# A two-layer encoder trunk: roots of the last head pair as a power on GpSimd, an early table load and halved gelu, four places in the planned order

## The chip, the cores and the metric

The kernel runs on one core of a Trainium2 chip. The metric is the time of one execution on the device, in microseconds (us). A core has five engines with a queue each, which run side by side and wait for one another through semaphores: TensorE (PE in the profile; its weight loads are shown apart as PEld), VectorE (DVE), ScalarE (ACT), GpSimd (POOL) and SyncE (SP), which here issues nearly all transfers (DMA) between main memory and the core. The instructions of one queue are executed in the order in which they stand there.

## The reference

The input is x, 1024 tokens by 1024 channels in float32. The trunk has two layers, each `x = x + mixer(RMSNorm(x))`, and a final RMSNorm. The first layer's mixer has two branches from one projection; the change lies mostly in them.

```python
def mixer_ab(h, w_in, ..., glu_w, glu_b, w_out):
    proj = h @ w_in
    u_s5, g_s5, q, k, v, g_ret = jnp.split(proj, cuts, axis=-1)
    y_s5 = s5_mixer(u_s5, ..., glu_w, glu_b)
    y_s5 = y_s5 * jax.nn.silu(g_s5)
    ...
    y_ret = retention(q, k, v).astype(h.dtype) * jax.nn.silu(g_ret)
    return jnp.concatenate([y_s5, y_ret], axis=-1) @ w_out
```

At its end, `s5_mixer` (a diagonal state-space recurrence) takes a gelu of its y and then a gated linear unit, the GLU of this text: `y = gelu(y); y = y * sigmoid(y @ glu_w + glu_b)`. `retention` turns q and k by position (rotary: `x1*cos - x2*sin`, `x1*sin + x2*cos`), forms decayed scores inside a chunk and a carried state between chunks for 8 heads, and normalises each head's output over its 128 channels, `(out - mu) * rsqrt(var + EPS)`. The second layer's mixer is a Conformer convolution: `a, b, g = split(h @ w_in)`, `u = a * sigmoid(b)`, a causal convolution of width 31 along the tokens, LayerNorm, `silu`, times `silu(g)`, and `@ w_out` (mm_oc in the kernel).

## The kernel before, in words

Channels lie on the 128 partitions and tokens in the free dimension, in two halves of 512. To keep float32's precision, each operand of a product is split into a high and a low part (names ending in h and l, xh and xl, wh and wl), and TensorE makes three products for one: L231 wh·xh, L232 wh·xl, L233 wl·xh (`mm3`; for v the same three stand at L1192 to L1194 and L1216 to L1218). A weight block of 128 x 1024 takes three steps: SP loads wf (512 KB, L218), ACT casts it to wh (L220), POOL or DVE subtracts to get wl (L221). There are three buffers for each. A block of the last layers is split once and its low part kept in main memory (`lo_woc`); the second half of the tokens then loads wl directly (`low_load`).

In time: the S5 kernel and the gated projections run to about 270 us, then four head **pairs** of retention (to about 560 us), with the S5 branch's gelu and the sums for the GLU woven in; then the GLU (about 530 to 630), the output projection, and the second layer to 1136.

For one pair, `retention` does this. `ret_proj` makes k and q (mm_k, mm_q) and turns them: SP loads a copy with halves swapped (kswp, qswp), POOL multiplies raw and swapped by the tables (L1158, L1160), DVE adds (L1161, krot and qrot). q's table, `ropeq`, has one buffer of 1 MB for all pairs, so the next pair's table (L1135) can be loaded only when the last qswp product has read the old one. `ret_values` (pair 0: `ret_values_wide`, for all heads, eight weight blocks v0_0_0 to v0_1_3) makes v, which ACT evacuates from the banks (L1195, L1220). `y_pass` takes two blocks of the S5 output per pair: SP loads yp (L1034), ACT takes the gelu (L1038), SP stores yn_d; DVE makes differences (L1046 to L1049), casts th (L1053), subtracts (L1054), and SP stores both as t_d (L1055, L1056). `glu_sums` loads blocks of the GLU's weight as gs (L1065), adds and subtracts them on DVE (L1069 to L1072) and stores ws_d (L1075). `ret_heads` makes the scores, the state, the outputs ro, their statistics (st, mv), the reciprocal root rs by `rsqrt` (ACT's Sqrt at L530 and DVE's reciprocal at L531), the normalised `on`, which TensorE transposes (rt, L1329), and the gated result grl, stored as yr_d.

The GLU is built from seven products of blocks over the sums and differences (a Strassen-like scheme), 14 weight blocks glu0 to glu13, whose operands are loaded as y11f, y21f, y22f (split on the core: casts at L1339) and yt1 to yt4 (loaded split, L1381). `gated` multiplies a product by tanh (sg, mm_glus, mm_gluy: L1416 on ACT; the sigmoid is written with it), POOL multiplies gate and y (yg, L1408). ACT has one set of function tables at a time; an ACT_TABLE_LOAD stands in its queue where Sqrt, gelu and tanh follow one another.

The order of each queue is not that of the text: a planner with a model of durations orders the program, and three things bind it. `tc.issue_after(ins)` queues what a block traces **on the engine of `ins`** behind `ins` (order only, no wait; on other engines it has no effect). `self.at(priority)` moves a piece. And the table `ORDER` (L41) lists pairs (engine, early, late): the late instruction, by tile name and number, is to be queued behind the early one, for example qswp_0's first product against a wl_v0 block.

## Time and profile before

| | |
|---|---|
| three runs | 1133.12, 1135.58, 1136.41 us; median 1135.58 |
| the profiled execution | 1138.03 us, of which span 1136.2 |
| TensorE clock granted | 0.999 |
| instructions in the span | 17205 |
| main memory | 182.53 MB read, 74.65 MB written, 226 GB/s over the span |

The span is the time from the first to the last instruction in the trace; 1.8 us of the execution lie around it. Busy times are shares of the span. A row of a timeline has start, length, engine, line, operation, tiles and, in brackets, how long the engine had been idle and what ended it; matmul ends are modelled, so starts are the better measure on TensorE.

### The profile page before, as it was taken

To read this page: it belongs to the slowest core of one execution; us is meant where nothing else is said; L and a number is where in the kernel's file an instruction comes from. 1 tells how busy PE (TensorE), PEld (TensorE's weight loads), DVE (VectorE), ACT (ScalarE), POOL (GpSimd) and SP (SyncE) were. 2 spreads that over 40 slices of the span, in tenths; PEclk is the share of its full clock that TensorE was granted. 3 is DMA by queue.
4 is the path that set the end of the run, shared out by engine and by line. 5 is a ranking of instruction groups with operands and counts; after the bars stand their busy time and mean duration, and the time that the engine had idled before them with its cause. 6 is when DMAs were issued, how large, how long until landed. Compare 5 with 4: busy or idle time off the path is not lost.

```text
span 1136.2 us, 17205 instructions
## 1 busy us (share of the span) xinstructions
PE 1117.1 (98%) x6278; PEld 978.9 (86%) x6278; DVE 828.1 (73%) x1470; ACT 498.0 (44%) x731; POOL 647.3 (57%) x456
## 2 busy tenths in 40 slices
PE   9999999999999999999999999999999999999997
PEld 7888888888888889898888888888888888888886
DVE  6973966777417469587569632599999899999734
ACT  6412433333223221323436523555535677446773
POOL 2059999888127344232475011589544568779863
PEclk9999999999999999999999999999999999999999
DMA  9345555553477866959998998565778755357965
GB/s 354 114 124 167 188 185 176 177 172 138 151 245 251 303 212 181 337 168 325 382 372 277 328 330 285 192 237 198 242 252 281 249 195 179 119 179 246 317 229 187
DMA packets 118181, 262.51 MB, mean 231 GB/s; under 512 B 10704, under 2 KB 42320, under 8 KB 117456
## 3 DMA queue, kind: packets, MB, share of 16 engines
q1 hardware_dynamic: 114640, 248.82, 64.9%
q10 hardware_dynamic: 3456, 12.58, 2.8%
q8 instruction: 49, 0.80, 0.3%
q14 instruction: 36, 0.29, 0.1%
HBM read 182.53 MB, written 74.65 MB: 226 GB/s over the span
## 4 chain that ended last, share of the span: by engine, by line
PE 73%; DMA 13%; DVE 7%; ACT 3%; issue 2%; POOL 1%; SPq 1%; POOLq 0%; DVEq 0%; ACTq 0%
PE mm_g L231 7%; PE mm_g L232 7%; PE mm_g L233 7%; PE mm_wo L231 5%; PE mm_wo L233 5%; PE mm_wo L232 5%; PE mm_a L233 2%; DMA yp<-y_d 2%; PE mm_b L232 2%; PE mm_a L231 2%; PE mm_b L233 2%; PE mm_a L232 2%; PE mm_b L231 2%; PE mm_oc L233 2%; PE mm_oc L231 2%; PE mm_oc L232 2%
## 5 line engine op out<-in xcount | busy, mean ns | idle before, releaser
L1626 DVE SCALAR_TENSOR_TENSOR cv<-u,convw,cv 128x512 f32<-128x512 f32 x390 | 267.7, 749 | 5.4 <-ACT cv L1593 3.4
L1587 POOL TENSOR_TENSOR tp<-tp,tp 128x512 f32<-128x512 f32 x64 | 82.4, 1288 | 33.8 <-ACT tp L1586 32.9
L231 PE MATMUL mm_g<-xh,wh_g 128*128 128x512 f32 x256 | 97.9, 382 | 0.0
L232 PE MATMUL mm_g<-xl,wh_g 128*128 128x512 f32 x256 | 97.0, 379 | 0.0
L233 PE MATMUL mm_g<-xh,wl_g 128*128 128x512 f32 x256 | 95.7, 379 | 0.0
L492 POOL TENSOR_TENSOR s1q<-s1q,s1q 128x512 f32<-128x512 f32 x12 | 17.1, 1424 | 79.1 <-ACT s1q L487 79.1
L1586 ACT ACTIVATE tp<-u,convw 128x512 f32<-128x512 f32 x64 | 45.3, 718 | 34.4 <-POOL tp L1587 33.6
L231 PEld LDWEIGHTS mm_g<-xh,wh_g 128*128 128x128 f32 x256 | 48.8, 191 | 6.8 <-issue 0.2
L442 DVE TENSOR_TENSOR gt<-mm_g,R 128x512 f32<-128x512 f32 x32 | 21.9, 686 | 44.7 <-PE mm_g L233 44.6
L233 PEld LDWEIGHTS mm_g<-xh,wl_g 128*128 128x128 f32 x256 | 48.4, 189 | 6.9
L232 PEld LDWEIGHTS mm_g<-xl,wh_g 128*128 128x128 f32 x256 | 48.4, 189 | 6.6
L221 POOL TENSOR_TENSOR wl_glu<-wf_glu,wh_glu 128x1024 fp32r<-128x1024 f32 x14 | 34.0, 2432 | 33.1 <-ACT wh_glu L220 33.1
L233 PE MATMUL mm_oc<-zh,wl_woc 128*128 128x512 f32 (+1 forms) x144 | 51.0, 357 | 1.2 <-DMA wl_woc<-lo_woc 1.2
L232 PE MATMUL mm_oc<-zl,wh_woc 128*128 128x512 f32 (+1 forms) x144 | 51.2, 356 | 0.0
L231 PE MATMUL mm_oc<-zh,wh_woc 128*128 128x512 f32 (+1 forms) x144 | 50.7, 363 | 0.0
L232 PE MATMUL mm_u<-xl,wh_u 128*128 128x512 f32 x128 | 48.3, 381 | 0.7 <-DVE xl L365 0.7
L233 PE MATMUL mm_a<-h1h,wl_ca 128*128 128x512 f32 x128 | 48.6, 380 | 0.3 <-DMA wl_ca<-lo_ca 0.3
L231 PE MATMUL mm_wo<-ysh,wh_wos 128*128 128x512 f32 x128 | 48.9, 382 | 0.0
L231 PE MATMUL mm_g<-h1h,wh_cg 128*128 128x512 f32 x128 | 48.9, 382 | 0.0
L232 PE MATMUL mm_wo<-ysl,wh_wos 128*128 128x512 f32 x128 | 48.5, 379 | 0.0
L233 PE MATMUL mm_wo<-ysh,wl_wos 128*128 128x512 f32 x128 | 48.5, 379 | 0.0
L233 PE MATMUL mm_b<-h1h,wl_cb 128*128 128x512 f32 x128 | 48.5, 379 | 0.0
(533 smaller groups left out, 3601.9 us busy)
## 6 DMA issues: line engine op xcount, KB each, us to landing
wf_g<-w_ab SPq DMA_DIRECT2D x16, 512.0 KB, 5.0
wf_wos<-w_out SPq DMA_DIRECT2D x16, 512.0 KB, 4.5
wf_wor<-w_out SPq DMA_DIRECT2D x16, 512.0 KB, 5.6
wf_cb<-w_c SPq DMA_DIRECT2D x16, 512.0 KB, 4.8
wf_ca<-w_c SPq DMA_DIRECT2D x16, 512.0 KB, 5.6
wf_woc<-w_out_c SPq DMA_DIRECT2D x16, 512.0 KB
wf_v<-w_v SPq DMA_DIRECT2D x12, 512.0 KB
wf_cg<-w_c SPq DMA_DIRECT2D x11, 512.0 KB, 4.5
```

Source lines behind the costliest of these rows:

```text
L221: self.low_made = lo[i].tensor_tensor(wl[:].rearrange(fl)[:, c], wf[:, c], h.bitcast(F32), op=ALU.subtract)
L231: nc.tensor.matmul(ps, wh[:, kb, :], xh, start=start, stop=False, **more)
L232: nc.tensor.matmul(ps, wh[:, kb, :], xl, start=False, stop=False, **more)
L233: self.last_mm = nc.tensor.matmul(ps, wl[:, kb, :], xh, start=False, stop=stop, **more)
L442: nc.vector.tensor_tensor(nat(gt[:, c]), un(ps[:]), nat(self.R[:, c]), op=ALU.mult)
L492: nc.gpsimd.tensor_tensor(a, a, sq[:], op=ALU.add)
L1586: nc.scalar.mul(sk[:], u[:, k:k + HALF], cw[:, nb, k:k + 1])
L1587: gp.tensor_tensor(s0[:], s0[:], sk[:], op=ALU.add)
L1626: v.scalar_tensor_tensor(dst[:], *tap, accs_[i][:], op0=ALU.mult, op1=ALU.add)
```

## The change

Five things are written:

- `rsqrt` for pair 3 (`pool=pair == 3`): the four rs of the last pair (heads 6 and 7, two halves) are made by a multiply-add on DVE and a power of −0.5 on POOL, 128x4 each, instead of Sqrt on ACT and reciprocal on DVE. `rsqrt` now returns the POOL instruction there, so `last_rs` of pair 3 is one of POOL's, and the two `issue_after(self.last_rs.ins)` in the GLU (the first weights, the first tanh) no longer tie anything on ACT.
- For pairs 1 to 3 gelu's table is loaded right behind the last root of the pair before (`preload_act_table_set` in `issue_after`).
- For pairs 1 to 3 the gelu of 128x1024 is two of 128x512.
- `ORDER`: the first qswp product of pair 0 is tied behind the split of block v0_1_0 in place of v0_0_1; the split ysl2_0 on DVE behind the sum gu2_2; the third matmul of mm_oc2 (second half of tokens), the first that reads its wl, behind the ninth of mm_oc0.

```diff
     ('DVE', ('cv6_0', 23), ('h1l0_1', 0)),
-    ('Pool', ('qswp_0', 0), ('wl_v0_0_1', 0)),
+    ('Pool', ('qswp_0', 0), ('wl_v0_1_0', 0)),
+    ('DVE', ('ysl2_0', 0), ('gu2_2', 0)),
+    ('PE', ('mm_oc2_1_0', 2), ('mm_oc0_1_0', 8)),
 )
...
             nc.vector.tensor_scalar(dst, src, scale, EPS, op0=ALU.mult, op1=ALU.add)
-            nc.gpsimd.tensor_tensor(dst, dst, self.mhalf[:, :dst.shape[1]], op=ALU.pow)
+            return nc.gpsimd.tensor_tensor(dst, dst, self.mhalf[:, :dst.shape[1]], op=ALU.pow)
...
-                nc.scalar.activation(yn[:], yt[:].rearrange("p i m -> p m i"), AF.Gelu_apprx_tanh)
+                for m in ((slice(0, 64), slice(64, P)) if k in (1, 2, 3) else (slice(0, P),)):
+                    nc.scalar.activation(yn[:, m], yt[:, :, m].rearrange("p i m -> p m i"), AF.Gelu_apprx_tanh)
...
                     held.enter_context(self.tc.issue_after(self.last_rs.ins))
+                    nc.scalar.preload_act_table_set("gelu_apprx_tanh_and_others")
...
-                self.last_rs = self.rsqrt(rs[:], mv[:, :, 1])
+                self.last_rs = self.rsqrt(rs[:], mv[:, :, 1], pool=pair == 3)
```

What the planner makes of it is more than the diff says. Lines are two to four higher in the changed kernel (L218 is L220, L1160 is L1164, and so on).

**POOL, the values of pair 0.** Splits wl_v of the eight weight blocks and the rotary products qswp. Before:

```order
L221 TENSOR_TENSOR wl_v_0_2_3409<-wf_v_0_2_3407,wh_v_0_2_3408 128x1024
L1160 TENSOR_TENSOR qswp_3370<-qswp_3370,ropeq_3238 128x512 x2
L221 TENSOR_TENSOR wl_v_0_3_3439<-wf_v_0_3_3437,wh_v_0_3_3438 128x1024
L221 TENSOR_TENSOR wl_v_1_0_3469<-wf_v_1_0_3467,wh_v_1_0_3468 128x1024
L221 TENSOR_TENSOR wl_v_1_1_3499<-wf_v_1_1_3497,wh_v_1_1_3498 128x1024
```

Now:

```order
L223 TENSOR_TENSOR wl_v_0_2_3409<-wf_v_0_2_3407,wh_v_0_2_3408 128x1024
L1164 TENSOR_TENSOR qswp_3370<-qswp_3370,ropeq_3238 128x512
L223 TENSOR_TENSOR wl_v_0_3_3439<-wf_v_0_3_3437,wh_v_0_3_3438 128x1024
L223 TENSOR_TENSOR wl_v_1_0_3469<-wf_v_1_0_3467,wh_v_1_0_3468 128x1024
L1164 TENSOR_TENSOR qswp_3370<-qswp_3370,ropeq_3238 128x512
L223 TENSOR_TENSOR wl_v_1_1_3499<-wf_v_1_1_3497,wh_v_1_1_3498 128x1024
```

One of the two products has moved behind two splits. On DVE, one of the two qrot sums moved with it, behind the second th cast.

**SP, the same stretch.** wf_v_1_1 to wf_v_1_3 are the last v weights, ropeq the next pair's table, wf_k the next pair's k weight. Before:

```order
L218 DMA wf_v_1_1_3497<-w_v 128x1024
L1135 DMA ropeq_3897<-rope_q 128x2048
L1065 DMA gs_0_3383<-w_glu 128x2x512
L218 DMA wf_v_1_2_3536<-w_v 128x1024
L1075 DMA ws_d<-gs_1_3393 256x1x512
L1055 DMA t_d<-th_0_3674 128x1024
L218 DMA wf_v_1_3_3566<-w_v 128x1024
L1056 DMA t_d<-yn_3662 128x1024
L1075 DMA ws_d<-gs_1_3392 256x1x512
L1075 DMA ws_d<-gs_0_3383 256x1x512
L1075 DMA ws_d<-gs_0_3382 256x1x512
L218 DMA wf_k_3596<-w_ab 128x1024
```

Now:

```order
L220 DMA wf_v_1_1_3497<-w_v 128x1024
L220 DMA wf_v_1_2_3536<-w_v 128x1024
L1078 DMA ws_d<-gs_1_3393 256x1x512
L1058 DMA t_d<-th_0_3674 128x1024
L220 DMA wf_v_1_3_3566<-w_v 128x1024
L1059 DMA t_d<-yn_3662 128x1024
L1078 DMA ws_d<-gs_1_3392 256x1x512
L1139 DMA ropeq_3897<-rope_q 128x2048
L1058 DMA t_d<-th_0_3679 128x1024
L1068 DMA gs_0_3383<-w_glu 128x2x512
L1059 DMA t_d<-yn_3667 128x1024
L220 DMA wf_k_3596<-w_ab 128x1024
```

The table and gs_0 went from ahead of wf_v_1_2 to behind wf_v_1_3, ahead of wf_k; two ws_d went behind wf_k, two t_d ahead of it.

**ACT, pair 3's roots and the first tanh.** gu are copies of the GLU's first products, wh_glu casts of its weights, sg the first tanh. Before:

```order
L1443 COPY gu_1_5521<-mm_glu_5529 128x512
L530 ACT_TABLE_LOAD
L530 ACTIVATE rs_0_5356<-mv_0_5347,epst 128x4
L530 ACTIVATE rs_0_5374<-mv_0_5365,epst 128x4
L530 ACTIVATE rs_1_5410<-mv_1_5401,epst 128x4
L530 ACTIVATE rs_1_5428<-mv_1_5419,epst 128x4
L220 CAST wh_glu_5579<-wf_glu_5578 128x1024
L1416 ACT_TABLE_LOAD
L1416 ACTIVATE sg_0_5600<-mm_glu_5528,hgb 128x512
```

Now:

```order
L1447 COPY gu_1_5530<-mm_glu_5538 128x512
L222 CAST wh_glu_5588<-wf_glu_5587 128x1024
L1420 ACTIVATE sg_0_5609<-mm_glu_5537,hgb 128x512
L222 CAST wh_glu_5638<-wf_glu_5637 128x1024
L1420 ACTIVATE sg_0_5633<-mm_glu_5538,hgb 128x512
```

Both table loads and the four roots have left ACT. Their successors, four TENSOR_TENSOR of 128x4 at L530, stand on POOL behind the first yg product and ahead of the split of this same wh_glu.

In pairs 1, 2 and 3 the load of gelu's table stands right behind the last root on ACT (pair 1: the same place as before; pair 2: four v evacuations earlier; pair 3: the same place, but without the wait for yp). In the GLU, SP's load of glu6 went from ahead of the eight yt4 loads to behind them, that of glu8 from ahead of one yg and the eight yt1 loads to behind them, and the last y22f and the first yr0f came ahead of the load of glu11. On TensorE, the first transposes rt of pair 3 stand four matmuls later; in mm_oc, six matmuls of the next block of zh and zl stand ahead of mm_oc2's first with wl.

## The prediction

> **What bounds the kernel now.** I read the page's table of engines first, then the waits of TensorE, longest first (engine, line and tile that waited, what it waited for, us in total, times, longest).

> ```profile
> PE 1117.1 (98%) x6278; PEld 978.9 (86%) x6278; DVE 828.1 (73%) x1470; ACT 498.0 (44%) x731; POOL 647.3 (57%) x456
> ...
> PE mm_glu L231 <- ACT sg L1416: 1.6, 1, 1.6
> PE mm_v L1217 <- POOL wl_v L221: 1.5, 2, 1.2
> PE mm_oc L233 <- DMA wl_woc<-lo_woc: 1.2, 1, 1.2
> PE mm_v L1192 <- ACT v L1195: 1.1, 1, 1.1
> ...
> PE mm_glu L231 <- ACT v L1195: 0.9, 1, 0.9
> PE mm_wo L231 <- ACT yr0h L1339: 0.9, 1, 0.9
> PE mm_glu L231 <- DVE mm_gluz L1477: 0.7, 1, 0.7
> ...
> PE mm_k L233 <- POOL wl_k L221: 0.6, 1, 0.6
> ```

> TensorE works 1117.1 of 1136.2 us and the diff leaves its 6278 matmuls as they are, so the change can only win these short waits or put new ones in their place. The eight rows shown sum to 8.5 us, and the edits aim at all of them but yr0h and, by their own words, wl_k. A 512-column matmul follows its predecessor every 0.2157 us though its row shows 0.38, so a wait of the list costs 0.15 to 0.25 us more than it says; below I use the distance between two starts, less 0.2157 (0.11 for 256 columns).

> **1. The rotary product of pair 0 (350 to 384 us).** Rows: start, length, engine, line, tile.

> ```profile
> 350.46 2.51 POOL L1160 TENSOR_TENSOR qswp<-qswp,ropeq 128x512 f32<-128x512 f32 x2 [1.40 <-DMA gs<-w_glu]
> 352.93 8.36 POOL L221 TENSOR_TENSOR wl_v<-wf_v,wh_v 128x1024 fp32r<-128x1024 f32 x3
> ...
> 354.19 0.38 PE L1216 MATMUL mm_v<-wh_v,xh 128*128 128x512 f32 x1
> 355.78 0.48 PE L1217 MATMUL mm_v<-wl_v,xh 128*128 128x512 f32 x1 [1.22 <-POOL wl_v L221]
> ...
> 372.26 1.05 ACT L220 CAST wh_v<-wf_v 128x1024 fp32r<-128x1024 f32 x1 [8.45 <-DMA wf_v<-w_v]
> 380.10 1.05 ACT L220 CAST wh_k<-wf_k 128x1024 fp32r<-128x1024 f32 x1 [6.79 <-DMA wf_k<-w_ab]
> ...
> 381.22 2.37 POOL L221 TENSOR_TENSOR wl_k<-wf_k,wh_k 128x1024 fp32r<-128x1024 f32 x1 [5.00 <-ACT wh_k L220]
> ...
> 383.64 0.48 PE L233 MATMUL mm_k<-xh,wl_k 128*128 128x512 f32 x1 [0.60 <-POOL wl_k L221]
> ...
> 372.78 7.22 DMA wf_k<-w_ab
> ...
> 374.00:384.00 10.00, 9.40 (x48) 8.01 (x47) 1.35 (x3) 3.52 (x6) 4.59 (x2) 1.00 1.03 383
> ```

> One of two qswp products (2.51 / 2 = 1.26 us) leaves the place ahead of wl_v_0_3 and goes behind wl_v_1_0. wl_v_0_3 then starts 1.26 us earlier, at 351.7, and is ready near 354.4 instead of 355.7: the wait of 355.78 − 354.19 − 0.22 = 1.38 us goes. The qswp is itself needed late, so its own delay is free.

> But TensorE's next lock in this stage is wl_k, and that one is set by SP's queue. Its chain has no slack: wf_k is issued at 372.78 and lands 7.22 us later (the chain of waits), ACT casts it at 380.10, POOL splits it from 381.22 to 383.59, TensorE goes on at 383.64. The rope table's load (ropeq, 1 MB) can't be issued before the second qswp has read the old table, so it moves from the head of this queue to behind the fourth weight of v, and with it gs_0. Between that weight and wf_k there stood t_d and three ws_d, all of 512 KB; now t_d, ws_d, the table (two such pieces), t_d, gs_0, t_d. With wf_k itself it is 5 pieces before and 8 now. In 374 to 384 the queue is full (share 1.03, 383 GB/s), which is 0.524 MB / 383 GB/s = 1.37 us a piece. Before, the five took from the cast of the fourth weight, 372.26, to that of wf_k, 380.10: 7.84 us. Now eight take 8 × 1.37 = 10.96, from a start that I let come 0.5 us earlier because wf_v_1_2 no longer queues behind the table: 371.7 + 11.0 = 382.7, against 380.0. With the same cast and split behind it TensorE resumes **2.7 us later** than before; the 1.38 us won is lost inside that. Bounds: wf_k's issue moves up by about 0.9 us (two ws_d fewer ahead of it); if the queue had room for all that is new, −0.9. A piece more: +4.1.

> **2. Pair 2's gelu (465 to 470 us) and 3. pair 3's (500 to 530 us).**

> ```profile
> 465.84 1.28 ACT L1038 ACT_TABLE_LOAD   x1 [4.97 <-DMA yp<-y_d]
> 467.14 1.98 ACT L1038 ACTIVATE yn<-yp 128x1024 f32<-128x1024 f32 x1
> 469.02 1.19 ACT L1195 ACTIVATE v<-mm_v,Rtok 128x256 f32<-128x256 f32 x3
> ...
> 500.15 1.28 ACT L1038 ACT_TABLE_LOAD   x1 [0.91 <-DMA yp<-y_d]
> 501.44 2.05 ACT L1038 ACTIVATE yn<-yp 128x1024 f32<-128x1024 f32 x1
> ...
> 528.39 0.62 ACT L1339 CAST y21h<-y21f 128x512 fp32r<-128x512 f32 x1 [6.08 <-DMA y21f<-yn_d]
> 528.92 0.83 ACT L1195 ACTIVATE v<-mm_v,Rtok 128x256 f32<-128x256 f32 x2
> ```

> In pair 2 ACT idles 4.97 us for yp, then loads the table, and the v evacuation that TensorE's bank waits for stands behind load and gelu. The load now fits into that idle time: 1.28 us off a wait of 1.13 in the list (1.30 by starts). Two halves instead of one whole add some 0.1 us (an estimate: the 1.98 of one whole is my only row). I take **−1.15**, bounds −1.3 and −0.8.

> In pair 3 the last root ends 0.91 us ahead of the load, so the gelu moves up by 0.9 us plus at most the rest of 1.28. What waits on it is long: yn_d, the t_d and y21f loads, then the cast y21h at 528.39, which holds v at 528.92 and so TensorE (0.94 in the list, 1.10 by starts). Queue and chain move together: **−0.9**, bounds −0.3 (if the full queue from 512 us on keeps its own pace) and −1.1.

> [...]

> **4. Pair 3's roots (545 to 556 us).**

> ```profile
> 546.41 0.30 ACT L530 ACTIVATE rs<-mv,epst 128x4 f32<-128x4 f32 x1
> ...
> 553.08 1.28 ACT L1416 ACT_TABLE_LOAD   x1
> 554.37 0.69 ACT L1416 ACTIVATE sg<-mm_glu,hgb 128x512 f32<-128x512 f32 x1
> ...
> 547.07 1.28 POOL L1408 TENSOR_TENSOR yg<-yg,yn 128x512 f32<-128x512 f32 x1
> ...
> 551.84 1.04 PE L1329 MATMUL rt<-ident,on 128*128 128x128 f32 x8
> ...
> L1829 POOL TENSOR_TENSOR fo<-x,RF 128x256 f32<-128x256 f32 x4 | 2.8, 726 | 4.9 <-ACT RF L1819 4.9
> ```

> With no Sqrt left, the Sqrt table's load, four roots and the tanh table's load leave ACT; sg can start when its product is there, instead of 554.37. TensorE's longest wait (1.6 in the list, 1.75 by starts) goes: **−1.75**. The price moves to POOL: four powers of 128x4 behind yg, which ends at 548.35, and ahead of the next wl_glu. The trace has no power. From 128x256 at 0.73 and 128x512 at 1.28 the line through no columns stands at 0.18 us, which is the lower bound; 1.28 us, seven times that and the length of a whole 128x512 product, is my upper one. At 1.28 the first two powers end at 550.9, the `on` products of DVE about 1.5 us later, and the first transposes, which ran from 551.84 and stand four matmuls (0.86) later now, begin at 552.7: no wait. I take 0.3 us, near the rows' small end, and nothing for it.

> **5. The GLU's weights and 6. its tail (557 to 601 us).**

> ```profile
> 557.00:592.00 35.00, 35.00 (x168) 30.71 (x167) 20.04 (x25) 12.82 (x19) 25.44 (x15) 1.00 1.03 383
> ...
> 568.21 7.94 DMA yt1h<-t_d
> 576.21 5.32 DMA yg<-gs_d
> ...
> 576.11 1.04 ACT L220 CAST wh_glu<-wf_glu 128x1024 fp32r<-128x1024 f32 x1
> ...
> 577.23 2.45 POOL L221 TENSOR_TENSOR wl_glu<-wf_glu,wh_glu 128x1024 fp32r<-128x1024 f32 x1 [0.33 <-ACT wh_glu L220]
> ...
> 585.01 0.38 PE L233 MATMUL mm_glu<-yt4h,wl_glu 128*128 128x512 f32 x1
> ...
> 590.19 0.62 ACT L1339 CAST y22h<-y22f 128x512 fp32r<-128x512 f32 x1 [2.99 <-DMA y22f<-yn_d]
> ```

> TensorE never waits from 557 to 592, but the DMA queue is full there. The planner now puts the ninth weight, glu8, behind one yg and the eight yt1 loads. The first of these lands at 568.21 + 7.94 = 576.15, the load behind the last at 576.21 + 5.32 = 581.53: 5.38 us for eight, 0.67 each, so glu8 lands some 6 us later, near 580.9 (0 to 0.9 earlier with step 3). Cast 1.04 and split 2.45 give 583.5 to 584.4. Before, TensorE wanted this split at 585.01 and it was ready at 579.68; having won 0.9 + 1.75 in steps 3 and 4, which the full queue doesn't follow, it wants it at 582.4. So of that gain **+1.4** comes back (bounds 0 and +2.5). In return the last y22f goes out about 3 us earlier; its cast at 590.19 holds DVE's chain up to mm_gluz, TensorE's 0.7 (0.88 by starts): **−0.9** (0 to −1.0).

> **7. mm_oc (1084 us).**

> ```profile
> 1081.08 4.19 DMA wl_woc<-lo_woc
> ```

> The third matmul on this weight waits for 1085.27. Six others now stand ahead of it, 6 × 0.2157 = 1.29 us, whose operands another chunk has ready by then: **−1.3** (−0.8 to −1.4).

> Sum: +2.7 − 1.15 − 0.9 − 1.75 + 1.4 − 0.9 − 1.3 = **−1.9 us**. The profiled execution took 1138.03, 2.45 us above the median of the runs, 1135.58; so a profile of the changed kernel near 1136.1, and a median of 1135.58 − 1.9 = **1133.7 us**.

> **The rivals.** A, the give-backs don't come: the rope table finds room, since the queue was only part busy before 374, and glu8 is in time. Then terms 1 and 5 are −0.9 and 0, and the sum is −6.9: 1128.7 us. For it speaks that only two waits, each inside one queue, stand against it; against it the share of 1.03. B, the power is dear on POOL. At 3 us each the first two end at 548.35 + 6 = 554.35, the first transposes wait about 3 us (555.8 for 552.7); powers three and four end at 560.35, and `on` and the second transposes lose 2.2 us more: +5.3, in sum +3.4, or 1139.0 us. From there on it is slower. Nothing but the rows' linear shape speaks against it, since no row has this operation. C, the queues swallow the rest: the table costs +4.1, glu8 +2.5 and pair 3 wins 0.3 only; +1.2 in sum, 1136.8 us. D, the planner's move does less than it says, as in pair 2 if yp should land later: within 1 us of the forecast, so it is counted with it.

> **Numbers.** Differences under 0.3% (3.4 us) are what the three runs, 1133.12 to 1136.41, can't tell from no change. Forecast with D 0.48, A 0.26, C 0.14, B 0.12. The forecast's own range is −5 to +1 us; I put 0.14 of its 0.48 past −3.4. Faster 0.26 + 0.14 = 0.40, same 0.34 + 0.12 (C without its worst) = 0.46, slower 0.12 + 0.02 = 0.14. The range goes from A's 1128.7, a little below, to C with half of B: 1128.3 to 1138.0 us.

> **What would show it.** Right: no wait of mm_v on wl_v at 355; wf_k landing near 382.7 and mm_k waiting about 4 us for wl_k; no table load between 545 and 557 and sg at once behind its product; a new wait of mm_glu on wl_glu (or wh_glu) near 582; none of mm_oc on lo_woc. Wrong: mm_k waiting less than 1 us (rival A), a power's row over 1.3 us with rt waiting (B), waits of mm_glu over 3 us in all (C). A wait at a place that none of these edits touches would make the sum itself wrong.

## The result and the profile after

| | before | changed |
|---|---|---|
| runs | 22, 1131.82 to 1138.12 us | 22, 1133.20 to 1143.46 us |
| median | 1134.56 us | 1138.45 us |
| ratio, 95% interval | 1 | 1.0034 (1.0024 to 1.0044) |
| mean granted clock over the runs | 0.9987 (the 30 runs beside e1 to e4) | 0.9968 |
| the profiled execution, its span | 1138.03, 1136.2 | 1140.53, 1138.8 |

The change makes the kernel slower by 0.34%, where 1133.7 us were forecast. The waits of TensorE in the changed kernel (what it waited for, us in total, times, longest):

```profile
PE mm_k L233 <- ACT wh_k L222: 3.2, 1, 3.2
PE rt L1333 <- DVE on L1325: 1.5, 1, 1.5
...
PE mm_k L235 <- POOL wl_k L223: 1.0, 1, 1.0
PE mm_glu L233 <- ACT v L1199: 0.7, 1, 0.7
...
PE mm_oc L235 <- DMA wl_woc<-lo_woc: 0.6, 1, 0.6
...
PE mm_glu L235 <- POOL wl_glu L223: 0.2, 1, 0.2
...
PE mm_v L1196 <- ACT v L1199: 0.2, 1, 0.2
```

Gone are the waits on wl_v, sg, mm_gluz and yr0h; new are one of 3.2 us on wh_k and one of 1.5 us of the transposes. That is less waiting in sum than before, and yet the span is 2.6 us longer, so part of the loss is not in this list. The chain of waits, then the timeline of TensorE behind the late weight:

```profile
373.99 8.68 DMA wf_k<-w_ab
...
383.86 0.48 PE L233 MATMUL mm_k<-xh,wh_k 128*128 128x512 f32 x1 [3.18 <-ACT wh_k L222]
...
386.30 0.79 PE L235 MATMUL mm_k<-xh,wl_k 128*128 128x512 f32 x1 [0.97 <-POOL wl_k L223]
386.88 0.63 PE L233 MATMUL mm_k<-xh,wh_k 128*128 128x512 f32 x1
387.31 0.63 PE L234 MATMUL mm_k<-xl,wh_k 128*128 128x512 f32 x1
387.74 0.63 PE L235 MATMUL mm_k<-xh,wl_k 128*128 128x512 f32 x1
...
393.53 0.66 PE L1259 MATMUL kv<-v,kt 128*64 128x128 f32 x8
```

wf_k lands at 373.99 + 8.68 = 382.67, as predicted. But behind the wait the matmuls follow each other every 0.43 us instead of 0.2157. Windows of 4 us show it too (the column before the last two is the granted clock):

```profile
380.00:384.00 4.00, 0.82 (x7) 0.51 (x5) 3.37 (x5) 1.23 (x2) 0.11 (x1) 1.00 1.09 369
384.00:388.00 4.00, 2.92 (x10) 2.06 (x11) 0.69 (x1) 3.07 (x5) 3.10 (x2) 0.68 1.03 393
388.00:392.00 4.00, 4.00 (x10) 3.10 (x10) 0.00 (x0) 1.99 (x2) 2.39 (x2) 0.50 0.75 230
392.00:396.00 4.00, 4.00 (x49) 3.38 (x49) 1.22 (x4) 0.33 (x1) 1.47 (x1) 0.96 0.92 320
```

TensorE ran at half clock until about 392 us. The clock missing in the three windows from 384, weighed by their lengths (0.32 x 4 + 0.50 x 4 + 0.04 x 4), is 3.4 us of work, so the clock stood at half for 6.8 us, a part of it idle. The same products, from this third one of mm_k (386.30) to the first kv (393.53), take 7.23 us; in the kernel before they take 4.30 (383.64 to 387.94). Where the difference of the two profiles arises is read from the start of the matmul with the same number, counted from the program's beginning, in both:

| place | before | changed | difference |
|---|---|---|---|
| values of pair 0, behind wl_v_0_3 | 357.40 | 355.52 | −1.9 |
| behind mm_k's first bank, pair 1 | 388.11 | 393.70 | +5.6 |
| behind pair 2's gelu | 470.53 | 474.72 | +4.2 |
| behind the first sg | 556.08 | 558.26 | +2.2 |
| at the second transposes of pair 3 | 558.46 | 562.48 | +4.0 |
| GLU, behind mm_gluz | 602.84 | 605.73 | +2.9 |
| the last matmul | 1129.96 | 1132.45 | +2.5 |

The gelu's table and the powers, first on ScalarE's timeline, then on GpSimd's and TensorE's:

```profile
503.28 1.28 ACT L1105 ACT_TABLE_LOAD   x1
504.71 2.13 ACT L1041 ACTIVATE yn<-yp 128x512 f32<-128x512 f32 x2
...
552.11 2.01 POOL L530 TENSOR_TENSOR rs<-rs,mhalf 128x4 f32<-128x4 f32 x2
558.75 1.98 POOL L530 TENSOR_TENSOR rs<-rs,mhalf 128x4 f32<-128x4 f32 x2 [4.63 <-DVE rs L529]
...
562.48 0.77 PE L1333 MATMUL rt<-ident,on 128*128 128x128 f32 x5 [1.47 <-DVE on L1325]
```

DVE's `on` products wait for the first powers:

```profile
553.17 1.37 DVE L1325 TENSOR_SCALAR on<-ro,mv,rs 128x128 f32<-128x128 f32 x4 [2.22 <-POOL rs L530]
```

A power of 128x4 takes 1.0 us. Pair 3's halves take 2.13 together where the whole took 2.05.

### The profile page after: what moved, and what is told of

Its sections match the earlier page's. It is cut to its first block, busy times and chain, and to the rows that moved or that the text cites. A ratio compares the mean times of both kernels' runs of the same rounds, so it can differ in the third digit from the quotient of the medians.

```text
span 1138.8 us, 17216 instructions
## 1 busy us (share of the span) xinstructions
PE 1121.3 (98%) x6278; PEld 981.2 (86%) x6278; DVE 828.2 (73%) x1470; ACT 494.8 (43%) x731; POOL 652.0 (57%) x460
## 4 chain that ended last, share of the span: by engine, by line
PE 74%; DMA 12%; DVE 6%; issue 2%; ACT 2%; POOL 1%; SPq 1%; POOLq 0%; DVEq 0%; ACTq 0%
PE mm_g L233 7%; PE mm_g L234 7%; PE mm_g L235 7%; PE mm_wo L235 5%; PE mm_wo L234 5%; PE mm_wo L233 5%; DMA yp<-y_d 3%; PE mm_b L234 2%; PE mm_b L233 2%; PE mm_a L233 2%; PE mm_a L235 2%; PE mm_b L235 2%; PE mm_a L234 2%; PE mm_oc L235 2%; PE mm_oc L234 2%
## 5 line engine op out<-in xcount | busy, mean ns | idle before, releaser
L233 PE MATMUL mm_g<-xh,wh_g 128*128 128x512 f32 x256 | 97.9, 382 | 0.0
L233 PEld LDWEIGHTS mm_g<-xh,wh_g 128*128 128x128 f32 x256 | 48.8, 191 | 6.8 <-issue 0.2
L233 PE MATMUL mm_oc<-zh,wh_woc 128*128 128x512 f32 (+1 forms) x144 | 50.8, 363 | 0.0
L233 PE MATMUL mm_wo<-ysh,wh_wos 128*128 128x512 f32 x128 | 49.0, 383 | 0.0
L233 PE MATMUL mm_g<-h1h,wh_cg 128*128 128x512 f32 x128 | 48.9, 382 | 0.0
L233 PE MATMUL mm_a<-h1h,wh_ca 128*128 128x512 f32 x128 | 48.5, 379 | 0.0
```

What stands on the lines that cost most here:

```text
L233: nc.tensor.matmul(ps, wh[:, kb, :], xh, start=start, stop=False, **more)
```

## The experiments

Three theories run through them. **C**: the late weight makes TensorE wait, and the wait lowers its clock. **W**: only the waiting counts. **R**: the roots and the reordered GLU are the cause.

**e1, the qswp entry alone, and e2, all the rest.** e1 is the kernel before with

```diff
-    ('Pool', ('qswp_0', 0), ('wl_v0_0_1', 0)),
+    ('Pool', ('qswp_0', 0), ('wl_v0_1_0', 0)),
```

and e2 the changed kernel with the same line turned back.

> The kernel before with the one entry for qswp moved and nothing else. Theory C (the late weight wf_k of pair 1 makes TensorE wait over 3 us, and that wait lets its clock fall to half for some 6 us): the wait of mm_k on wh_k comes as in the changed kernel, 3 us, behind it 512-column matmuls 0.43 us apart up to about 392 us, and the whole is 4 to 6 us slower than before (ratio 1.0035 to 1.005). Rival R (the powers on GpSimd and the GLU's reordered loads cost the time, and the clock is the same with or without them): within 1.5 us of before.

> The changed kernel with only the qswp entry put back. Theory C: no wait of mm_k over 1 us, clock 0.998 or more, 2 to 3.5 us faster than before (ratio 0.997 to 0.998), since what is left of the change won 3.1 us by the end of its profile behind 394 us. Rival R: still slower than before, 1 to 4 us.

e1: median 1139.24 against 1134.86, ratio 1.0049 (1.0029 to 1.0069), mean clock 0.9967. e2: 1133.13, 0.9990 (0.9978 to 1.0002), mean clock 0.9989. Theory R falls: the qswp entry alone costs as much as the whole change loses. e1's profile differed from the expectation in one point: mm_k waited 0.47 and 0.98 us there, not 3, at full clock (1.00 from 376 to 400 us), and the half clock (0.50 from 524 to 526) stood behind a 2.2 us wait of mm_v at 523 us. What e2 wins is half of what was expected, and its interval holds 1.

**e3 and e8, the weight ahead of the table.** The changed kernel with one entry more, in e8 with both of these:

```diff
     ('Pool', ('qswp_0', 0), ('wl_v0_1_0', 0)),
+    ('SP', ('ropeq_1', 0), ('wf_k1', 0)),
+    ('SP', ('gs1_0', 0), ('wf_k1', 0)),
```

> The changed kernel with one more entry: the rope table's load (1 MB) behind wf_k on SP, so two pieces of 1.37 us less ahead of wf_k. Theory C: wf_k lands near 380.0 instead of 382.7, mm_k waits under 2 us in all, the clock stays at 1.00 from 384 to 394 us, and the whole is 2 to 4 us faster than before. A theory W (only the waiting counts, the clock doesn't hang on it): 2.7 us less than the changed kernel, so about 1 us slower than before, with the half clock still there.

> e3 with the load of gs_0 (512 KB, one piece) behind wf_k as well. If every piece ahead of wf_k costs 1.37 us: wf_k lands 1.4 us earlier than in e3 (378.1), the wait of mm_k on wl_k (1.2 us by starts in e3) is gone, and the time is 0.5 to 1.2 us under e3's, ratio to before 0.998 to 0.999. If the time hangs on later stages alone: as e3, 0.9993.

e3: 1133.35 against 1134.86, 0.9993 (0.9980 to 1.0006); in its trace wf_k's cast starts at 378.19 and mm_k waited 1.2 us at full clock (1.00 from 376 to 400 us). e8: 1133.39 against 1135.14, 0.9980 (0.9963 to 0.9996); the cast starts at 377.51 and mm_k did not wait. So the loss passes through SP's queue: qswp may stay where the change put it if the table isn't ahead of the weight. The gain of e3 is smaller than expected, as that of e2.

**e9 and e10, only the weight later.** The kernel before with one entry that changes two rows of SP and no other engine; in e10 the number is 2 in place of 3, one row:

```diff
     ('Pool', ('qswp_0', 0), ('wl_v0_0_1', 0)),
+    ('SP', ('wf_k1', 0), ('t_d', 3)),
```

> The kernel before with nothing changed but two rows of SP's queue: wf_k behind the two t_d stores of 512 KB that stood behind it (qswp stays where it was). It lengthens the wait for pair 1's k weight by two pieces, 2.7 us, and touches nothing else. Theory C (a wait of some 3 us halves TensorE's clock for several us): mm_k waits 2.5 to 4 us, half-clock matmuls behind it, mean clock 0.997 or less, and 4 to 6 us slower than before (1.0035 to 1.005). Theory W (only the waiting counts): 2 to 2.7 us slower (1.002) at an unchanged clock.

> The same with one t_d store ahead of wf_k in place of two: 1.37 us more wait. Theory C: the wait stays under 2.3 us, the clock seldom falls, and it is 0.7 to 1.5 us slower than before (1.0005 to 1.0015). Theory W: half of e9, 1 to 1.4 us slower.

e9: 1137.45 against 1134.06, 1.0029 (1.0012 to 1.0046), mean clock 0.9983. e10: 1134.47, 1.0011 (0.9993 to 1.0028), clock 0.9984. Two pieces of 512 KB ahead of one weight cost about 3 us in the runs, with nothing else moved. Here theory W does better: the kernel before stood at 0.9986 beside it, so hardly any of this went through the clock. But both theories expected mm_k to wait, and e9's profile (1135.58, in the faster half of its runs) does not show that: wf_k's cast starts at 377.37 there, earlier than in the first profile of before (380.10), and mm_k waits 0.2 us; its longest waits are two of 1.7 us of mm_v, at 467 and 521 us. Where the slower runs of e9 lose their time was not seen.

**e5, the kernel before a second time.**

> The kernel before once more, for a second profile. Its first profiled execution, 1138.03 us, lies at the top of its 30 runs (1130.6 to 1138.2, median 1134.9). If its waits there (1.75 on sg, 1.40 on lo_woc, 1.38 on wl_v, 1.30 and 1.10 on v, 1.04 on yr0h, by starts) are fixed by the program, they come again within 0.2 us each; if they are an accident of that execution's transfers, some shrink to under half, and the terms of the prediction that rested on them were too large.

1135.57 us. Its waits, and the place of qswp on GpSimd's timeline:

```profile
PE mm_glu L231 <- ACT sg L1416: 1.7, 1, 1.7
PE mm_oc L233 <- DMA wl_woc<-lo_woc: 1.4, 1, 1.4
PE mm_glu L231 <- ACT v L1195: 1.2, 1, 1.2
...
PE mm_v L1192 <- ACT v L1195: 0.7, 1, 0.7
...
346.18 2.51 POOL L1160 TENSOR_TENSOR qswp<-qswp,ropeq 128x512 f32<-128x512 f32 x2 [0.39 <-DMA qswp<-qraw]
```

The waits on wl_v (1.38) and wl_k (0.85) are not in it at all: qswp ran 4.3 us earlier and was through long before the split was wanted, and wf_k's cast started at 374.85, not 380.10. The waits on sg, lo_woc and v are there again. The very wait that the moved qswp was to remove comes in some executions only.

**e11, e12, e15, the changed kernel three times more**, as it stands.

> The changed kernel once more, for a second profile, since its 22 runs reach from 1133 to 1143. If the late weight is fixed by the program: wf_k lands at 382 to 383 again, mm_k waits over 3 us, and the half clock follows. If DVE and GpSimd fall out of step differently from execution to execution (in the trace of e1 the first t_d goes out at 360.5, in that of the changed kernel at 365.7): wf_k lands near 379 in some executions, the wait is about 1.5 us, and the execution takes 1134 to 1136.

> The changed kernel a third time, for a third profile; as the second. The time of each profiled execution should go with the length of the wait of mm_k in it: 1134 to 1136 where the wait is under 2 us in all, 1138 or more where it is over 3.

> The changed kernel a fourth time. So far: wait of mm_k 3.34 + 1.22 us with half clock for 6 us (1140.5), 1.24 + 1.22 with 3.4 us of half clock (1136.7), 1.05 + 1.22 with none (1134.1). Theory C: the three go together here too, and an execution over 1138 us shows half clock at some wait of 2 us or more. Theory W: an execution over 1138 us without half clock.

The waits of mm_k and the window from 384 to 388 us, in the order e15, e11, e12:

```profile
PE mm_k L233 <- ACT wh_k L222: 2.0, 1, 2.0
...
384.00:388.00 4.00, 3.36 (x8) 2.74 (x9) 0.18 (x1) 1.41 (x2) 2.94 (x2) 0.57 0.82 296
```

```profile
PE mm_k L233 <- ACT wh_k L222: 1.1, 1, 1.1
...
PE mm_k L235 <- POOL wl_k L223: 1.0, 1, 1.0
...
384.00:388.00 4.00, 4.00 (x12) 3.20 (x12) 0.00 (x0) 1.19 (x2) 2.35 (x1) 0.61 0.78 243
```

```profile
PE mm_k L235 <- POOL wl_k L223: 1.0, 1, 1.0
PE mm_k L233 <- ACT wh_k L222: 0.9, 1, 0.9
...
384.00:388.00 4.00, 4.00 (x24) 3.27 (x24) 0.00 (x0) 1.11 (x2) 2.37 (x1) 1.00 0.67 224
```

Four profiles of one program, wf_k landing at 382.67, 381.01, 379.80 and 379.72; waits of mm_k on wh_k of 3.2, 2.0, 1.1 and 0.9 us; half clock for 6.8, 3.4, 3.4 and 0 us; and 1140.53, 1136.19, 1136.65 and 1134.06 us. The three go together, but for the order of the middle two. The price of the half clock can be read alone: from mm_k's third product to the first kv, the same products take 7.23, 5.87, 5.99 and 4.30 us, so 2.9, 1.6, 1.7 and 0 us more than the 4.30 of before.

None of the three new profiles came over 1138 us, but the recorded runs bear on theory W. Of the changed kernel's 22, the two slowest, 1142.47 and 1143.46 us, have a mean clock of 0.997 and 0.998, while one of 1136.70 has 0.995. A clock of 0.998 leaves room for one period of 3.4 us at most (e13, with one, shows 0.998, and so does e12, with none: half clock behind the last matmul, 1.7 us of it inside the span in before and 2.4 in the changed kernel, lowers the mean too). A straight line through the 22 gives 0.9 us of time for each us of missing clock, and leaves about three quarters of the spread to something else. So the clock costs about what it is short of, and it is not all that makes these runs slow.

**e4, e6, e13, e14, the wait filled with work.** The changed kernel with products of ones into mm_k's bank, which its first product overwrites:

```diff
                 ps = self.bank(f"mm_{nm}{pair}_{h}", aux=False)
+                for _ in range(12 if (nm, pair, h) == ("k", 1, 0) else 0):
+                    nc.tensor.matmul(ps[:, :P], self.ones[:], self.ones[:], start=True, stop=True)
```

In e4 the planner put the state's products kv ahead of mm_k. From e6 on an entry `('PE', ('kv0_0', 0), ('mm_k1_0', 35))` holds them behind mm_k's first bank.

> The changed kernel with twelve extra products of ones into mm_k's own bank, ahead of its first product (which overwrites them): about 2.6 us of work for TensorE inside the wait for wh_k; transfers and waits are otherwise as they were. Theory C: mm_k's first real product starts as late as in the changed kernel (about 383.9 us), but the products behind it are 0.216 us apart, not 0.43, and the whole is about 3 us faster than the changed kernel (ratio to before 0.999 to 1.002). Theory W: as slow as the changed kernel, 1.0025 to 1.0045.

> As e4 (twelve products of ones, about 2.6 us, ahead of mm_k's first product in the changed kernel), with the state's products kv tied behind mm_k's first bank, as they stand in the changed kernel, since in e4 they had moved ahead of it. Theory C (the wait lowers the clock): mm_k's real products start as late as in the changed kernel, the idle time of TensorE there is under 1.5 us in one piece, mean clock over the runs 0.998 or more against the changed kernel's 0.9968, and the time 1.5 to 3 us under the changed kernel's: ratio to before 1.0005 to 1.002. Theory W (only the waiting counts): 1.003 to 1.004 with the same mean clock as the changed kernel.

> The kernel of e6 (filled wait, order kept) for another profile. Its 12 runs fell into two groups: 4 of 1134.1 to 1136.6 us at a clock of 0.998 to 1.0, and 8 of 1140.9 to 1144.8 at 0.996 to 0.997; its profile was of the first group. In an execution of the second group, theory C1: the half clock stands at mm_k again (384 to 392 us), because the weight came so late that 2.6 us of filling didn't cover it; theory C2: mm_k runs at full clock and a later wait of 2 us or more, made by the transfers that the table's load pushed back (sp on qrot near 435, as in e4's profile, or mm_v near 468 or 522), has the half clock behind it.

> The same kernel a third time, in case e13 falls into the first group; the theories as in e13.

Both expectations of a gain failed. e4: 1144.53, 1.0078 (1.0052 to 1.0104), clock 0.9963. e6: 1141.81, 1.0045 (1.0025 to 1.0066), clock 0.9972, in two groups: 4 runs from 1134.1 to 1136.6 at 0.998 to 1.0, and 8 from 1140.9 to 1144.8 at 0.996 to 0.997. In all three profiles of this kernel (e6 1134.70, e13 1136.63, e14 1135.37) mm_k ran at full clock (products 0.2157 us apart in e6, a clock of 1.00 from 380 to 392 us in e13 and e14); the unfilled kernel did so in one of four. But in e13 the clock fell later, behind mm_v (waits, then windows):

```profile
PE mm_v L1199 <- ACT v L1202: 2.8, 2, 2.2
...
522.00:526.00 4.00, 1.79 (x14) 1.60 (x14) 3.10 (x3) 1.97 (x4) 1.95 (x2) 0.94 0.82 293
526.00:530.00 4.00, 4.00 (x25) 4.00 (x25) 2.43 (x3) 0.00 (x0) 0.00 (x0) 0.64 1.03 410
```

So work in the wait kept the clock at that place in all three, and in one of them it fell at a later long wait. No profile fell in the group over 1140 us; where its clock falls, and whether that is what makes it slow, stays open.

**e7, e16 and e17, the powers.** e7 is e2, and e16 is e8, each with `pool=pair == 3` taken out again; e17 is the kernel before with that argument (and the `return`) alone.

> e2 (the changed kernel with the qswp entry put back) with pair 3's roots on ScalarE again, so only the early gelu table, the halves and the two entries on ysl2 and mm_oc2 remain. If the powers are worth the wait on sg (1.75 us) less the new wait on the first transposes (1.6 us in the changed kernel's profile): within 0.5 us of e2. If they win the whole 1.75: 1.5 to 2 us slower than e2, so ratio to before about 1.000.

> e8 (rope table and gs_0 behind wf_k) with pair 3's roots on ScalarE again: the candidate for the best version. If the powers are worth nothing, as e7 against e2 says: equal to e8, ratio to before 0.9975 to 0.9985, so 2 us faster than before. If the powers win their 1.75 us in this kernel: 0.9995.

> The kernel before with pair 3's roots as powers on GpSimd and nothing else, as the direct measure of that part. Theory D (the wait on sg, 1.75 us, is replaced by a wait of the transposes on the normalised outputs, 0.7 to 1.6 us, and by wl_glu later): 0 to 1 us faster than before, ratio 0.999 to 1.000. As predicted with no wait and glu8's 1.4 us back: 0.3 to 0.5 us faster. If powers are the change's other cost: slower than before by 1 us or more.

e7: 1133.78 against 1135.14, 0.9985 (0.9973 to 0.9996). e16: 1130.71 against 1133.64, 0.9975 (0.9962 to 0.9988), the best of all. e17: 1134.80, 1.0008 (0.9997 to 1.0019). The powers win nothing by themselves, and both kernels without them are at least as fast as with them. e17's waits say why:

```profile
PE mm_v L1192 <- ACT v L1195: 2.7, 2, 1.4
PE mm_glu L231 <- DVE gu L1463: 1.6, 2, 0.9
...
PE rt L1329 <- DVE on L1321: 0.9, 1, 0.9
```

The wait on sg is gone; transposes wait for `on`, and the GLU for DVE's sums (gu), which in the two profiles of before they did not.

## Why the prediction was wrong, point by point

**Step 1 (qswp) failed, and by its consequence, not its size.** The landing of wf_k was forecast at 382.7 and came at 382.67, and TensorE resumed at 386.30 against 383.64, 2.66 us later where 2.7 were forecast. The step ended there, as if a wait cost its own length: TensorE's clock was nowhere in the sum. In the changed kernel's profile it stood at half behind the wait, and by the first kv the delay had grown from 2.7 to 5.6 us. Changed kernel against e2, which differ in this entry alone, the means are 1138.32 and 1133.26: 5.1 us. The mean clocks 0.9968 and 0.9989 account for 0.0021 x 1137 = 2.4 of it (an estimate, since the clock is given to three places); 2.7 are left for waiting. In the changed kernel's own profiles that clock was lost at mm_k in three of four. The split is an estimate from means, and e9 lost 3 us almost without the clock.

That the landing came to a hundredth is in part luck. The sum priced eight pieces at 1.37 us each, though the five of before had taken 7.84 us from cast to cast, 1.57 each. From the cast of v's fourth weight to that of wf_k the eight took 11.3 us in this profile and 12.3, 13.5 and 13.7 in e15, e11 and e12, which began earlier and landed at 381.01, 379.80 and 379.72.

A second thing in the same step: the 1.38 us "won" and the 0.85 us wait of mm_k were rows of one execution, 1138.03, at the top of the 30 runs of before. In e5 both are zero. There the move of qswp had nothing to win.

How long the half clock lasts and when it comes can be read from the traces. It stood for 6.83 us in the changed kernel's profile (385.45 to 392.28) and for 3.4 in e11 (383.74 to 387.16), so for two and for one piece of 3.413 us, and 512-column matmuls followed each other every 0.43 us in it. In all 19 kept traces the clock falls a whole number of 3.413 us after it came up: 378.88 us, 111 of them, in the changed kernel, e11 and e15, and 1129.81 us, 331 of them, behind the last matmul of before. The wait ahead of a fall was not always as long as one such piece: 2.2 us at 523 in e1 and e13 were enough.

What was needed can be read by cutting the traces into windows of that length, counted from where the clock came up, and adding up TensorE's busy rows in each. Short of the program's end the clock fell behind six windows, in which TensorE was busy for 1.20 (e13), 1.31 (e1), 1.36 (changed kernel), 1.36 (e15), 1.65 (e11) and 1.73 us (e4) of 3.41. It fell behind none in which TensorE was busy for 1.74 us or more; the nearest are two of e9, 1.74 and 1.77, each with one wait of 1.7 us. The windows of e11 and e4 (fell), then of e12 and e9 (did not), with TensorE's busy time behind the length:

```profile
380.33:383.74 3.41, 1.65 (x7) 1.06 (x8) 1.17 (x2) 3.41 (x6) 2.36 (x1) 1.00 1.04 360
434.53:437.94 3.41, 1.73 (x20) 1.42 (x18) 3.38 (x3) 0.00 (x0) 1.86 (x1) 1.00 0.93 264
380.72:384.13 3.41, 2.13 (x10) 1.46 (x11) 0.73 (x2) 3.40 (x6) 2.35 (x1) 1.00 1.05 366
519.57:522.98 3.41, 1.74 (x16) 1.61 (x15) 2.96 (x3) 1.36 (x3) 1.81 (x2) 1.00 0.89 344
```

So in these traces the clock fell where TensorE was idle for about half of such a window, in one piece or in several (ends of matmuls are modelled, so the limit is good to a few hundredths at best). It also decides between e11 and e12, whose waits of mm_k were nearly alike (1.1 + 1.0 and 0.9 + 1.0 us): their windows lay differently, and that of e12 kept 2.13 us of work.

**Steps 2 and 3 (gelu) were right in kind.** Pair 2's wait of 1.1 us is gone in the changed kernel's profile (0.15 us in e11), and between mm_k and there the kernel gained 1.4 (forecast 1.15); in e5 that wait was 0.65, so a part of the gain was the execution's. Pair 3's fell from 0.9 to 0.7 (0.4 to 0.8 in the other three), not by its whole, and in three of the four profiles a new wait on v of 0.2 to 1.0 us stands ahead of it, at 523 to 526 us. The load stands directly behind the last root (503.28), but the chain over yn_d and y21f kept its pace: the cast y21h starts 29.7 us behind the start of the roots in both kernels (498.68 to 528.39, 502.70 to 532.43).

**Step 4 (powers) failed in the sum's term "no wait".** The price of a power, 1.0 us, lay inside the bounds taken (0.18 to 1.28), though three times the value chosen. But at 1.28 "no wait" was also claimed, and the transposes waited 1.5 us (562.48; 0.5 to 1.3 in the other three profiles). What was left out is DVE's own queue: the `on` products wait at its head for the power, and the statistics of the second half stand behind them, so its roots come late as well (second pair of powers at 558.75, 4.63 us idle before). The step's −1.75 was about 0 (e17, e7, e16).

**Step 5 (glu8)** cost next to nothing in place of 1.4: TensorE came to that product at 588.88 us, where the step had 582.4, and waited 0.2 us. In e3 and e8, where TensorE comes earlier, waits of 0.9 and 1.0 us by starts on wl_glu end at 582.13 and 582.65, as forecast. **Step 6** was right: the wait on mm_gluz is gone in all four profiles of the changed kernel. **Step 7** was half right: 0.6 us of the wait on lo_woc stayed, 0.7 of 1.3 were won.

All but step 1 was forecast at −4.6 us; e2 measured −1.4 in the mean. Step 4 is a part of what is missing (e7, without it, is as fast as e2). The rest was not shown by an experiment; in e2's profile other waits stand in the place of those removed, 1.0 on yr0h, 0.9 on v, 0.7 on wl_v and 0.4 on wl_glu. The profiles alone look better than the runs: from the first kv of pair 1 to the last matmul, before took 742.0 and 742.2 us and the changed kernel's four 737.6 to 739.1. But e10, which leaves all of that as it was, took 739.6 there, so such differences between single profiles are partly those of executions.

**The rivals.** B, the slower one, named the right sign and the wrong place. C, the queues, named the right place with +1.2 us, and had no clock in it either. The statement that a wait of mm_k of about 4 us would show step 1 right was itself the sign of what was missed: 2.2 us had half clock behind them in e1 and e13.

## What to carry to other kernels

A wait of the bounding matrix engine was not priced by its length alone here: in the changed kernel's profile TensorE resumed 2.7 us late, and its products behind that took 2.9 us longer. Where waits left it idle for about half of 3.4 us, in six of the 19 traces, the clock fell behind them, so ask what it does there; in the changed kernel that came to about as much again as the waiting, in e9 to hardly anything. Take the waits to be removed from several profiles, and drop those that come and go. When an instruction is moved, look at the buffer that it frees: here 1.3 us of GpSimd work held back 1 MB, which then stood in the queue ahead of the next weight; two entries for that queue and leaving the powers out (e16) made a loss of 0.34% a gain of 0.25%.
